# A mixed mLSTM and forgetting-attention step on one core: forget pages issued by GpSimd inside the q/k stage, one weight group rounded a step sooner, last outputs stored as whole rows

## The chip, the cores and the metric

The kernel runs on one core of a Trainium2 chip. The metric is the device time of one execution in microseconds; the median of the timed runs is compared. Engines are named as the profile names them: PE is TensorE (PEld its weight loads), DVE is VectorE, ACT is ScalarE, POOL is GpSimd, SP is SyncE (SPq its queue of DMA issues).

## The reference

One inference step of a two-layer decoder: an mLSTM layer and a layer of forgetting attention, each followed by a SwiGLU FFN, all in float32, for a prompt of 1024 positions (with 16 meta tokens ahead) and a decode batch of 8 x 8 positions. Cut to what the change touches:

```python
def mlstm_mixer(xn, C0, n0, m0, lead, w_in, b_ig, b_fg, mh_g, w_out):
    p = xn @ w_in                       # q | k | v | output gate | input gate | forget gate
    ...
    li = softcap(gi.astype(f32) + b_ig.astype(f32)).transpose(0, 2, 1)
    lf = jax.nn.log_sigmoid(softcap(gf.astype(f32) + b_fg.astype(f32))).transpose(0, 2, 1)
    h, state = mlstm_sequence(q, k, v, li, lf, state0, lead)
    h = rmsnorm(h.transpose(0, 2, 1, 3), mh_g)
    out = (h.reshape(B, T, HV).astype(xn.dtype) * jax.nn.sigmoid(og)) @ w_out
    return out, state
...
y = rmsnorm(h, prm['norm_final'])
```

The attention layer reads, for the decode batch, a paged cache: `page_table` (8 x 4) gives the pages of `cache_k`, `cache_v` and `cache_logf`; a page of `cache_logf` is 128 positions x 16 heads of log-forget values, whose running sums enter the attention scores.

## The kernel before

Positions form 9 tiles (`TT`: 80, then 8 of 128) and three groups of tiles (`TG`: 336, 384, 384 columns). Float32 products are made of three matmuls of a fast type: weights and activations are split into a high part (rounded by ACT, `whi`, `xh`) and a low part (the rest, by DVE, `wlo`, `xl`), and `mm3` (L193 to L195) multiplies high x high, high x low and low x high.

**The values stage** (`values_a`) is written out by hand: TensorE, SyncE, DVE and ACT run in the order of the code. Its loop over `i` has 9 + `LAG` steps, `LAG` = 5. Step `i` multiplies tile `i` by the weights of column group 0 (`values(0, i)`), and, from step 5 on, tile `i` - 5 by those of group 3 (`values(3, i - 5)`, 272 columns: 256 of v and 16 of the gates). `fetch(c, z)` loads half `z` of group `c` (`wraw`), `halve(c, z, ks)` rounds the quarters `ks` of that half: for each an ACT instruction (L665) and a DVE one (L666), and behind the last quarter of a half of group 3 the split of the gates' columns `gw` (L271, L272). Group 3's four pairs of quarters are rounded in steps 2 to 5.

**The q/k stage** (`phase_a`) has 24 steps `x`, one for each of 8 blocks of 128 columns of w_in and each group of positions. A step is 24 matmuls into `mmA` (a pool of two banks), an eviction by ACT into one of three buffers `stg` (L921), and a store to `qkD` from GpSimd's queue (L922). Each block's weights are loaded by SyncE (`load_w`, L256), rounded by ACT (L259) and DVE (L260). Between the steps stand:
- `rec_prep`, the work on the gates' rows: behind step 1 and behind step 4 TensorE transposes rows (`rps`, L1101, two banks) that ACT copies (`li`, `lf`, L1103); the rows of step 4 start a chain over DVE (scans `bA`, `mA`), ACT and DVE again, with stores from GpSimd: `out_p_m`, `out_s_m` (L1114, L1115), `eD` (L1120), and at its end `wD` (L1128). Behind step 9 TensorE transposes the results (`tps`, L1143, `wps`, L1147 and L1148).
- `cache_loads`: the page table is loaded, 32 registers are filled from it (L1011), and 32 pages of `cache_logf` are loaded by SyncE (L1013), four to a yield.
- `cache_prep`, at step 14: TensorE transposes the pages (`csps`, L1024), ACT copies (L1025), DVE sums (L1027), and GpSimd stores eight times `csE` (L1030). The loads of the state (`C`, `n`, L1308, L1310) wait for those stores.
- `wo_out`, at steps 6, 9, 12, 15 and 18: a block of w_out is loaded, rounded and stored (`woD`, L878) from GpSimd's queue.

Here TensorE alone runs in the order of the code; the order of the other engines is found by a scheduler when the program is built, and the registers of the pages are filled at the head of SyncE's program.

**The end** (`Tail`): the last three tiles of y_prompt are transposed back into two banks each, scaled by ACT (right half) and DVE (left half) and stored by SyncE in six stores of 128 x 512; the source of a store is four pieces of 128 columns of `H`.

## Time and profile before

| what | value |
|---|---|
| median of 3 timed runs | 2831.09 us (2831.01 to 2832.83) |
| profiled execution | 2833.03 us, of which the span is 2831.2 us |
| mean granted clock of TensorE | 0.994 |
| TensorE busy | 2760.9 us, 98% |
| DVE, ACT, POOL busy | 63%, 42%, 30% |
| DMA moved | 474.03 MB, mean 167 GB/s |

A row of a timeline gives start and duration in us, then the engine, the line, the operation, what is written and what is read, and in brackets the idle time ahead of it with what ended it. TensorE's durations overlap (matmuls are pipelined), so the distance between two starts tells what a matmul costs. A row of stretches (windows) gives for each engine the busy time in us with the number of instructions, then the clock that TensorE was granted (1.00 is full), the busy share of the DMA engines and GB/s. A row of waits says who waited on whom: us in total, times, the longest. A row of one line gives count and shortest, median and longest duration in ns, and when the first and the last began. Registers, waits and DMA issues don't count as busy.

### The profile page before, as it was taken

How to read it: one execution, taken by the hardware profiler on the slowest of the kernel's cores; microseconds unless marked ns; L12 is line 12 of the kernel's file. 1: busy time of each engine (PE TensorE's matmuls, PEld its weight loads, DVE VectorE, ACT ScalarE, POOL GpSimd, SP SyncE). 2: the span in 40 equal slices, each digit the busy share in tenths (PEclk: the TensorE clock that was granted, in tenths of full speed). 3: DMA queues.
4: the chain of work that ended last, by engine and by line, in shares of the span. 5: the costliest groups of instructions: out<-in, count | busy, mean ns of one | idle time of the engine just before them, and what ended most of it. 6: DMA issues, size and time to landing. Idle time of an engine off the chain costs nothing. (4 is left out here: it accounts for less than half of the span.)

```text
span 2831.2 us, 60542 instructions
## 1 busy us (share of the span) xinstructions
PE 2760.9 (98%) x23543; PEld 2649.8 (94%) x23543; DVE 1797.8 (63%) x4025; ACT 1177.0 (42%) x2299; POOL 837.0 (30%) x1316
## 2 busy tenths in 40 slices
PE   8989999999999999999999999999999999999998
PEld 8989889999999999999999888777899999999998
DVE  4632565888887665563455444777388888765656
ACT  5422453432322333443444445777343323323345
POOL 3122233132332332124352202554313223323111
PEclk9989999999999999999999999999999999999999
DMA  6666547245554375545443676442524555527556
GB/s 197 170 186 172 144 125 254 91 145 164 174 172 144 115 247 171 194 143 174 139 170 131 234 277 227 153 143 86 157 80 131 175 174 165 161 90 233 182 194 214
DMA packets 438737, 474.03 MB, mean 167 GB/s; under 512 B 41158, under 2 KB 364994, under 8 KB 437426
## 3 DMA queue, kind: packets, MB, share of 16 engines
q1 hardware_dynamic: 388050, 321.30, 36.9%
q0 software_dynamic: 43904, 143.18, 15.3%
q10 hardware_dynamic: 6496, 5.68, 0.6%
q8 instruction: 185, 3.03, 0.5%
q14 instruction: 102, 0.84, 0.1%
HBM read 322.84 MB, written 147.21 MB: 166 GB/s over the span
## 5 line engine op out<-in xcount | busy, mean ns | idle before, releaser
L1614 PE MATMUL m<-xh,slot 128*128 128x276 f32 x2752 | 540.5, 290 | 1.8 <-ACT fs L1643 1.8
L1614 PEld LDWEIGHTS m<-xh,slot 128*128 128x128 f32 x2752 | 439.6, 188 | 3.6 <-ACT fs L1643 2.2
L1614 PE MATMUL m<-xl,slot 128*128 128x276 f32 x1376 | 397.1, 289 | 0.0
L1614 PEld LDWEIGHTS m<-xl,slot 128*128 128x128 f32 x1376 | 258.7, 188 | 0.0
L193 PE MATMUL tmps<-slot,xh 128*128 128x256 f32 (+2 forms) x864 | 243.1, 281 | 0.0
L195 PE MATMUL tmps<-slot,xl 128*128 128x256 f32 (+2 forms) x864 | 240.6, 278 | 0.0
L194 PE MATMUL tmps<-slot,xh 128*128 128x256 f32 (+2 forms) x864 | 240.5, 278 | 0.0
L272 DVE TENSOR_TENSOR slot<-slot,slot 128x1024 fp32r<-128x1024 f32 x124 | 162.7, 1313 | 61.3 <-ACT slot L271 59.6
L271 ACT CAST slot<-slot 128x1024 fp32r<-128x1024 f32 x124 | 129.5, 1045 | 140.9 <-PE m L1614 111.7
L194 PEld LDWEIGHTS tmps<-slot,xh 128*128 128x128 f32 (+1 forms) x864 | 159.2, 184 | 0.1
L195 PEld LDWEIGHTS tmps<-slot,xl 128*128 128x128 f32 (+1 forms) x864 | 158.6, 184 | 0.0
L193 PEld LDWEIGHTS tmps<-slot,xh 128*128 128x128 f32 (+1 forms) x864 | 158.4, 183 | 0.2
L193 PE MATMUL mmA<-xh,whi 128*128 128x384 f32 (+1 forms) x384 | 135.7, 353 | 0.0
L194 PE MATMUL mmA<-xl,whi 128*128 128x384 f32 (+1 forms) x384 | 128.6, 335 | 0.0
L195 PE MATMUL mmA<-xh,wlo 128*128 128x384 f32 (+1 forms) x384 | 128.2, 334 | 0.0
L272 DVE TENSOR_TENSOR slot<-vA,slot 128x1024 fp32r<-128x1024 f32 (+1 forms) x59 | 82.2, 1396 | 32.6 <-ACT slot L271 31.5
L272 DVE TENSOR_TENSOR slot<-Ht,slot 128x1024 fp32r<-128x1024 f32 (+1 forms) x59 | 82.0, 1393 | 32.7 <-ACT slot L271 31.6
L271 ACT CAST slot<-Ht 128x1024 fp32r<-128x1024 f32 (+1 forms) x59 | 60.9, 1036 | 95.5 <-PE m L1614 86.5
L271 ACT CAST slot<-vA 128x1024 fp32r<-128x1024 f32 (+1 forms) x59 | 60.8, 1035 | 95.5 <-PE m L1614 86.5
L1718 DVE TENSOR_TENSOR ws<-ws 128x128 f32<-128x128 f32 x264 | 93.7, 355 | 8.9
L2865 ACT ACTIVATE s<-s,nb 128x272 f32<-128x272 f32 (+7 forms) x126 | 98.9, 786 | 0.0
L2900 ACT COPY th<-tp 128x768 f32<-128x768 f32 (+1 forms) x80 | 73.6, 920 | 53.6 <-PE tp L2892 30.5
(808 smaller groups left out, 8665.9 us busy)
## 6 DMA issues: line engine op xcount, KB each, us to landing
ws<-in_w_down SPq DMA_DIRECT2D x176, 128.0 KB, 2.7
sD<-ws SPq DMA_DIRECT2D x176, 128.0 KB, 2.2
slot<-sD SPq DMA_DIRECT2D x40, 512.0 KB, 4.4
slot<-in_w_gate_up SPq DMA_DIRECT2D x36, 512.0 KB, 3.9
kp<-in_cache_k SPq DMA_DIRECT2D x32, 512.0 KB, 6.2
vp<-in_cache_v SPq DMA_DIRECT2D x32, 512.0 KB, 5.1
vA<-in_w_gate_up SPq DMA_DIRECT2D x26, 512.0 KB, 4.5
Ht<-in_w_gate_up SPq DMA_DIRECT2D x26, 512.0 KB, 3.9
```

Of the source, the lines that this page charges most:

```text
L193: mm(ps, sh, mh, start=first, stop=False)
L194: mm(ps, sh, ml, start=False, stop=False)
L195: mm(ps, sl, mh, start=False, stop=last)
L271: self.nc.scalar.copy(hi, src)
L272: self.nc.vector.tensor_tensor(out=lo, in0=src, in1=hi.bitcast(F32), op=ALU.subtract)
L1614: nc.tensor.matmul(u.ps[h, b], w[p][:, k], x[q][:, k], start=first and k == i == 0, stop=k == 3 and i == 2, skip_group_check=True)
L1718: tt(out=o, in0=a, in1=b, op=ALU.subtract)
L2865: nc.scalar.activation(ss[z, u], ss[z, u], AF.Exp, bias=nb[:, z : z + 1], accum_out=sm[:, u, z : z + 1])
L2900: nc.scalar.copy(th.rearrange("p x z (u h q) -> p h (x z u) q", h=2, q=64)[:, :, :n], pt[:, :, :n])
```

## The change

Four edits. Lines in the following are those of the kernel after the change where an instruction has moved by a few lines (the eviction L921 becomes L922, its store L922 becomes L923).

1. `values_a`: group 3's pairs of quarters are rounded in steps 1 to 4, not 2 to 5.
2. `cache_loads`: the pages of `cache_logf` are loaded from GpSimd's queue, each behind a register load of GpSimd's own, two to a yield, from step 1 on (so in steps 1 to 16); GpSimd runs in the order of the code in this stage too; `cache_prep` moves from step 14 to step 18.
3. `page_at`: SyncE's registers for the pages of `cache_k` and `cache_v` are filled where they are first asked for. In the built program they stand where they stood, at the head of SyncE's queue.
4. `Tail.out`: the last three tiles are scaled into whole rows of 1024 and stored in one store each, two from SyncE's queue and the third from ACT's.

```diff
--- before.py
+++ after.py
@@ -791,8 +791,8 @@
                 keep(i + 2)
             if i + 6 < NT:
                 load(i + 6)
-            if 2 <= i < 6:
-                halve(3, i // 2 - 1, range(2 * (i % 2), 2 * (i % 2) + 2))
+            if 1 <= i < 5:
+                halve(3, (i - 1) // 2, range(2 * (1 - i % 2), 4 - 2 * (i % 2)))
             if i == 5:
                 fetch(1, 0)
                 fetch(1, 1)
@@ -882,6 +882,7 @@
 @_add(Net)
 def phase_a(self, vt):
     nc, I, O = self.nc, self.I, self.O
+    E = mybir.EngineType
     w_in = I["w_in_a"][0]
     qkD = self.dram.tile([8, P, T], F32, name="qkD")
     ogD = self.dram.tile([8, P, T], F32, name="ogD")
@@ -923,15 +924,16 @@
                     yield
 
         with self.pool("rowsA") as rp, self.pool("rowsAp", bufs=2, space=PSUM) as rpp, \
-                self.pool("cp") as cp, self.tc.manual_schedule(engines={mybir.EngineType.PE}):
+                self.pool("cp") as cp, self.tc.manual_schedule(engines={E.PE, E.Pool}):
             pages = self.cache_loads(cp)
             prep = self.rec_prep(kp, gates, rp, rpp)
             next(prep)
             for x, _ in enumerate(qk_out()):
                 if x in (1, 4, 9):
                     next(prep, None)
-                next(pages, None)
-                if x == 14:
+                if x:
+                    next(pages, None)
+                if x == 18:
                     self.cache_prep(*self.cache, rpp, "r")
                 if x % 3 == 0 and 5 < x < 21:
                     wo_out()
@@ -1002,16 +1004,14 @@
     nc, I = self.nc, self.I
     self.csE = self.dram.tile([NB, P, PAST], F32, name="csE")
     nc.sync.dma_start(self.ptab, I["page_table"].rearrange("b n -> (b n)").unsqueeze(0))
-    self.pages = []
+    self.pages = {}
     a, b = (cp.tile([P, 2 * PAST], F32, name=f"cp{x}") for x in range(2))
     lp = a[:, : NPG * NB * HB].rearrange("p (n b h) -> p n b h", n=NPG, b=NB)
-    for b_ in range(NB):
-        for n in range(NPG):
-            j = b_ * NPG + n
-            v = nc.sync.value_load(self.ptab[0:1, j : j + 1], min_val=0, max_val=I["cache_k"].shape[0] - 1)
-            self.pages.append(v)
-            nc.sync.dma_start(lp[:, n, b_, :], I["cache_logf"][bass.DynSlice(v, 1)].rearrange("a p h -> (a p) h"))
-        yield
+    for j in range(NB * NPG):
+        v = nc.gpsimd.value_load(self.ptab[0:1, j : j + 1], min_val=0, max_val=I["cache_k"].shape[0] - 1)
+        nc.gpsimd.dma_start(lp[:, j % NPG, j // NPG, :], I["cache_logf"][bass.DynSlice(v, 1)].rearrange("a p h -> (a p) h"))
+        if j % 2:
+            yield
     self.cache = lp, a[:, PAST:], b[:, :PAST], b[:, PAST:]
 
 
@@ -2063,17 +2063,11 @@
 
     def out(self, x, lo, hi):
         net, i = self.net, DONE[3][x]
-        nc, t0, t1 = net.nc, *TT[i]
-        for g, ps in enumerate((lo, hi)):
-            o = net.H[:, 4 * g : 4 * g + 4, t0:t1]
-            y, rr = ps.rearrange("p (k n) -> p k n", k=4), self.r[:, 1, x : x + 1]
-            if g:
-                nc.scalar.activation(o, y, AF.Copy, scale=rr)
-            else:
-                nc.vector.scalar_tensor_tensor(out=o, in0=y, scalar=rr, in1=net.sq[:, :512].rearrange(
-                    "p (k n) -> p k n", k=4), op0=ALU.mult, op1=ALU.mult)
-            nc.sync.dma_start(net.O["y_prompt"][0, (i - 1) * P : i * P, g * 512 : g * 512 + 512].rearrange(
-                "p (k n) -> p k n", k=4), o)
+        nc, rr = net.nc, self.r[:, 1, x : x + 1]
+        y = net.H[:, x, :D]
+        nc.scalar.activation(y[:, 512:], hi, AF.Copy, scale=rr)
+        nc.vector.scalar_tensor_tensor(out=y[:, :512], in0=lo, scalar=rr, in1=net.sq[:, :512], op0=ALU.mult, op1=ALU.mult)
+        (nc.scalar if x == 2 else nc.sync).dma_start(net.O["y_prompt"][0, (i - 1) * P : i * P], y)
 
     def finish(self, acc, groups):
         net = self.net
@@ -2494,12 +2488,21 @@
 
 
 @_add(Net)
+def page_at(self, j):
+
+    if j not in self.pages:
+        self.pages[j] = self.nc.sync.value_load(self.ptab[0:1, j : j + 1], min_val=0,
+                                                max_val=self.I["cache_k"].shape[0] - 1)
+    return self.pages[j]
+
+
+@_add(Net)
 def load_page(self, sk, b):
 
     self.page[b] = []
     for n in range(NPG):
         p = sk.tile([P, D], F32, name=f"kp{b}{n}", tag="kp", bufs=4)
-        self.nc.sync.dma_start(p, self.I["cache_k"][bass.DynSlice(self.pages[b * NPG + n], 1)].rearrange(
+        self.nc.sync.dma_start(p, self.I["cache_k"][bass.DynSlice(self.page_at(b * NPG + n), 1)].rearrange(
             "a p h d -> (a p) (h d)"))
         self.page[b].append(p)
 
@@ -2528,7 +2531,7 @@
         vp = []
         for n in range(NPG):
             p = s2.tile([P, D], F32, name=f"vp{b}{n}", tag="vp", bufs=6)
-            nc.sync.dma_start(p, I["cache_v"][bass.DynSlice(self.pages[b * NPG + n], 1)].rearrange(
+            nc.sync.dma_start(p, I["cache_v"][bass.DynSlice(self.page_at(b * NPG + n), 1)].rearrange(
                 "a p h d -> (a p) (h d)"))
             vp.append(p)
         Q = qb[b % 2]
```

What the order becomes on the engines. ACT in the values stage, in steps 4 and 5 (`xin` is the square of the rows of a later tile, `vA` an eviction, the last one that of group 3's first tile, `gw` the gates' columns), before:

```order
L751 ACTIVATE xin6_283,ss_136<-xin6_283 128x1024
L752 ACTIVATE rr_135<-ss_136,eps_67 128x1
L665 ACTIVATE whi_31_489<-wraw_14_260,gain_69 128x256 x2
L271 CAST xh_91<-xps_34_521 128x4x128
L271 CAST xh_91<-xps_35_526 128x4x128
L683 ACTIVATE vA_96<-tmps_33_495,rr_135 128x2x128
L751 ACTIVATE xin7_332,ss_136<-xin7_332 128x1024
L752 ACTIVATE rr_135<-ss_136,eps_67 128x1
L665 ACTIVATE whi_31_489<-wraw_14_260,gain_69 128x256 x2
L271 CAST whi_31_489<-gw_159 128x4x16
L683 ACTIVATE vA_96<-tmps_38_558,rr_135 80x2x128
```

and after:

```order
L751 ACTIVATE xin6_283,ss_136<-xin6_283 128x1024
L752 ACTIVATE rr_135<-ss_136,eps_67 128x1
L665 ACTIVATE whi_28_442<-wraw_14_260,gain_69 128x256 x2
L271 CAST whi_28_442<-gw_159 128x4x16
L271 CAST xh_91<-xps_34_527 128x4x128
L271 CAST xh_91<-xps_35_532 128x4x128
L683 ACTIVATE vA_96<-tmps_33_501,rr_135 128x2x128
L751 ACTIVATE xin7_332,ss_136<-xin7_332 128x1024
L752 ACTIVATE rr_135<-ss_136,eps_67 128x1
L683 ACTIVATE vA_96<-tmps_38_558,rr_135 80x2x128
```

The last rounding of group 3 (with `gw`) stood directly ahead of the first eviction of group 3; now it stands a step earlier, ahead of the two casts of `xh`.

ACT in the q/k stage about step 4 (`stg_112` and `stg_114` are the evictions of steps 3 and 4, `lf` the copies of the forget rows, `whi_133` the rounded fourth block of w_in), before:

```order
L259 CAST whi_126_2429<-wraw_125_2428 128x1024
L921 ACTIVATE stg_107_2053<-mmA_106_2028 128x384
L921 ACTIVATE stg_112_2127<-mmA_111_2102 128x336
L259 CAST whi_133_2534<-wraw_132_2533 128x1024
L921 ACTIVATE stg_114_2195<-mmA_113_2170 128x384
L1103 COPY lf_1870<-rps_115_2198 8x336
L1103 COPY lf_1870<-rps_116_2203 8x384
L1103 COPY lf_1870<-rps_117_2208 8x384
L1130 ACTIVATE stk_2230<-mA_1872 8x1104
```

and after:

```order
L259 CAST whi_126_2269<-wraw_125_2268 128x1024
L922 ACTIVATE stg_107_1993<-mmA_106_1968 128x384
L922 ACTIVATE stg_112_2047<-mmA_111_2022 128x336
L922 ACTIVATE stg_114_2095<-mmA_113_2070 128x384
L1103 COPY lf_1870<-rps_115_2098 8x336
L1103 COPY lf_1870<-rps_116_2103 8x384
L1103 COPY lf_1870<-rps_117_2108 8x384
L1130 ACTIVATE stk_2130<-mA_1872 8x1104
L259 CAST whi_133_2374<-wraw_132_2373 128x1024
```

The rounding of `whi_133` stood ahead of step 4's eviction and of the copies; now it stands behind them and behind `stk`.

GpSimd behind step 4's store (`cp` takes the pages, `ptab` is the page table, an ISA row works on registers), before:

```order
L922 DMA qkD<-stg_2195 128x384
L1115 DMA out_s_m<-mA 8x8x1
L1114 DMA out_p_m<-mA 8x1
L878 DMA woD_2599<-whi_2594 128x1024
L1120 DMA eD<-eA 8x1104
L922 DMA qkD<-stg_2311 128x384
L922 DMA qkD<-stg_2385 128x336
L1128 DMA wD<-wA 8x1104
L878 DMA woD_2599<-wlo_2595 128x1024
```

and after:

```order
L923 DMA qkD<-stg_2095 128x384
L1114 DMA out_p_m<-mA 8x1
L1115 DMA out_s_m<-mA 8x8x1
L1120 DMA eD<-eA 8x1104
L1128 DMA wD<-wA 8x1104
L1011 TENSOR_LOAD ptab
L1011 ISA x2
L1012 ISA
L1012 DMA cp_1946<-in_cache_logf 128x16
...
L923 DMA qkD<-stg_2191 128x384
```

The store `wD` now stands ahead of the stores of steps 5 and 6, and each step's pages stand between that step's store and the next one's. On SyncE the 32 page rows vanish, and the loads of w_in and w_out that stood behind them follow the earlier ones directly; on TensorE only the transposes `csps` move, four steps later.

## The prediction

> **What bounds the kernel now.** I read the page first. Its busy shares say that TensorE is the limit almost everywhere, so only what makes TensorE wait, or run slowly, can be won.
>
> ```profile
> PE 2760.9 (98%) x23543; PEld 2649.8 (94%) x23543; DVE 1797.8 (63%) x4025; ACT 1177.0 (42%) x2299; POOL 837.0 (30%) x1316
> ```
>
> The view of waits, asked for the first 46 us and for 140 to 255 us, gives two long waits of TensorE where the diff works: 2.7 us on ACT at L193, and 7.1 us on ACT at L1101. Both stand in the timelines below. The third place is the end of the program.
>
> **Part 1, group 3's weights a step sooner.** The timeline of TensorE at that wait, then two stretches of it (busy us of TensorE, its weight loads, DVE, ACT and GpSimd, then the granted clock and the DMA share):
>
> ```profile
> 34.82 0.29 PE L193 MATMUL tmps<-whi,xh 128*80 128x272 f32 x1
> ...
> 35.07 0.29 PE L195 MATMUL tmps<-whi,xl 128*80 128x272 f32 x1
> 38.11 0.51 PE L193 MATMUL tmps<-whi,xh 128*80 128x272 f32 x1 [2.75 <-ACT whi L271]
> ...
> 39.16 0.43 PE L193 MATMUL tmps<-whi,xh 128*80 128x272 f32 x1
> ...
> 39.62 0.43 PE L195 MATMUL tmps<-whi,xl 128*80 128x272 f32 x1
> ...
> 44.20 0.30 PE L195 MATMUL tmps<-whi,xl 128*128 128x256 f32 x1
> ```
>
> ```profile
> 20.00:24.00 4.00, 4.00 (x38) 4.00 (x37) 2.94 (x7) 3.17 (x8) 1.86 (x3) 1.00 0.98 326
> ...
> 40.00:44.00 4.00, 4.00 (x21) 4.00 (x20) 0.00 (x0) 0.63 (x2) 0.00 (x0) 0.50 0.26 77
> ```
>
> TensorE waits 2.75 us for the last quarter of the second half's weights, rounded in the same step that reads them. Behind it the granted clock is 0.50 (second stretch). Two starts take 0.46 us there (39.16 to 39.62) against 0.25 ahead of the wait (34.82 to 35.07). From 38.11 to 44.20, 6.1 us, the cold clock costs 6.1 x (1 - 0.25/0.46) = 2.8 us. Wait and cold clock together are 5.5 us.
>
> Rounded a step sooner, the weights are ready a step's length sooner, and what is added to step 1 must fit there (first stretch). ACT's roundings of two steps:
>
> ```profile
> 33.54 0.90 ACT L665 ACTIVATE whi<-wraw,gain 128x256 fp32r<-128x256 f32 x2
> ...
> 37.03 0.89 ACT L665 ACTIVATE whi<-wraw,gain 128x256 fp32r<-128x256 f32 x2
> ```
>
> A step is 3.5 us (33.54 to 37.03), more than the wait of 2.75. ACT is busy 3.17 of 4 us about step 1 and takes 0.89 more, DVE 2.94 and about as much: just full, without reserve. I leave 0.3 us of wait: **-5.2** (bounds 0, if the wait only moves, and -5.5).
>
> **Part 2, the pages off SyncE's queue.** The timelines of SyncE, ACT and TensorE at the 7.11 us wait:
>
> ```profile
> 130.63 18.31 SPq L1013 DMA_DIRECT2D cp<-in_cache_logf  x32
> 149.05 0.39 SPq L256 DMA_DIRECT2D wraw<-in_w_in_a  x1
> ```
>
> ```profile
> 153.31 1.04 ACT L259 CAST whi<-wraw 128x1024 fp32r<-128x1024 f32 x1 [9.56 <-DMA wraw<-in_w_in_a]
> ...
> 155.95 0.47 ACT L1103 COPY lf<-rps 8x384 f32<-8x384 f32 x1 [0.52 <-PE rps L1101]
> ```
>
> ```profile
> 147.21 0.78 PE L1101 MATMUL rps<-ident,lf_tm 80*8 80x80 f32 x6
> 155.11 0.80 PE L1101 MATMUL rps<-ident,lf_tm 128*8 128x128 f32 x3 [7.11 <-ACT lf L1103]
> ...
> 156.03 0.52 PE L194 MATMUL mmA<-xl,whi 128*128 128x384 f32 x1
> ...
> 156.99 0.52 PE L194 MATMUL mmA<-xl,whi 128*128 128x384 f32 x1
> ...
> 160.41 0.34 PE L193 MATMUL mmA<-xh,whi 128*128 128x384 f32 x1
> ...
> 160.93 0.34 PE L193 MATMUL mmA<-xh,whi 128*128 128x384 f32 x1
> ```
>
> SyncE issues 32 pages in a row for 18.31 us. The load of w_in behind them starts at 149.05, and ACT, whose next instruction is the rounding of that load, stands 9.56 us. The eviction of step 4 and the copies of the forget rows, which TensorE waits for, are queued behind it. After the change the load follows its predecessor directly, and on ACT the copies stand ahead of that rounding, so both causes go. What is late next is ACT's own eviction and first copies, done some 0.2 us after TensorE has its transposes: 6.9 of the 7.11 us go. The cold stretch goes with them: three matmuls take 0.96 us in it (156.03 to 156.99), 0.52 warm (160.41 to 160.93), so the 5.3 us from 155.11 to 160.41 cost 5.3 x (1 - 0.52/0.96) = 2.4. Together **-9.3** (bounds 0 and -9.5).
>
> **Part 3, the pages on GpSimd's queue: the unknown.** GpSimd now runs in program order: in step 4 it stops at the store of w (L1128), the end of a chain over DVE and ACT, and the remaining 26 pages, the qkD stores and the woD stores are queued behind. No page issue stands on GpSimd before, so I price it from rows of SyncE and of GpSimd's other DMAs:
>
> ```profile
> L922 POOL DMA_DIRECT2D qkD<-stg x24: 539/541/575, 132.6 to 242.5; - x24
> L1013 SPq DMA_DIRECT2D cp<-in_cache_logf x32: 332/333/1232, 130.6 to 148.6; - x32
> L1011 SPq TENSOR_LOAD <-ptab x9: 262/267/772, 38.2 to 43.6; - x9
> L1011 SPq TENSOR_LOAD <-ptab x32: 262/312/1044, 12.8 to 48.7; - x32
> DMA to landing us min/median/max: 1.6/1.8/3.8
> DMA to landing us min/median/max: 2.2/3.9/7.8
> ```
>
> The timelines of GpSimd, TensorE, ACT and SyncE further on:
>
> ```profile
> 167.65 0.80 POOL L1128 DMA_DIRECT2D wD<-wA  x1 [0.45 <-ACT wA L1127]
> 181.51 0.59 PE L1148 MATMUL wps<-tmA,selS 64*128 64x8 f32 x2
> 221.38 0.45 ACT L921 ACTIVATE stg<-mmA 128x336 f32<-128x336 f32 x1 [2.47 <-issue]
> 225.05 2.17 SPq L1310 DMA_DIRECT2D n<-in_state_n  x4
> 251.81 0.24 PE L1317 MATMUL n0p<-ident,n 32*128 32x32 f32 x1
> ```
>
> The two landing rows are the pages' (L1013) and the qkD stores' (L922). A GpSimd issue takes 0.54 us. A page adds registers, 18.31/32 - 0.333 = 0.24 on SyncE, and a register load, (43.6 - 38.2)/8 = 0.675 apart there. A page would cost 1.45 us. The low end is 0.54 + 0.24 + 0.26 = 1.04, with the shortest load and nothing behind it; the high end 2.2, if every load took the longest, 1.044 for the usual 0.3.
>
> Who waits: the transposes of the pages, now behind step 18 on TensorE, whose eviction is the row at 221.38. On the time axis of before, w goes out 11.2 us after the last copy of the rows (156.42 to 167.65). That copy now ends at about 148.9 (147.21 and 0.78 for the first transposes, 0.9 for the last group and its copy), so GpSimd is free again at 160.9. Until the last page it issues 26 pages, 12 qkD stores and 8 woD stores: 26p + 20 x 0.54. The page lands 1.8 us later. TensorE reaches the transposes at 221.38 less 9.3 and the 0.4 of the old transposes, 211.7. So there is no wait up to p = (211.7 - 1.8 - 160.9 - 10.8)/26 = **1.47 us**, and each 0.1 us above it costs 2.6 us. My value, 1.45, sits on that edge; I take **0** (bounds 0 and 26 x 0.73 = 19, with another 2.3 where the wait lets the clock fall). The evictions have three staging buffers. The first store after the stop, step 5's, is issued at 160.9 + 2.9 + 0.54 = 164.3 and lands at 168.2, at worst at 172.1; TensorE needs the next eviction from its buffer at 172.8, when it is through the small matmuls (181.51 + 0.6 - 9.3). That just holds. The csE stores and the state loads that wait for them come four steps later, some 4 x 8 x 0.52 = 16.6 us; the last state loads, issued until 227.2, are then issued at 243.8 and first used at 251.81, so their landing is hidden by 8 us, and if not, TensorE waits at L1317 for the rest.
>
> Beside this, GpSimd's DMAs land later while DVE is busy, as the store out_s_m shows, which was issued during the scans (its timeline and landing, the windows view, and a rounding on DVE):
>
> ```profile
> 157.30 0.61 POOL L1115 DMA_DIRECT2D out_s_m<-mA  x1 [1.72 <-DVE mA L1112]
> DMA to landing us min/median/max: 7.4/7.4/7.4
> 156.00:160.00 4.00, 4.00 (x14) 4.00 (x14) 4.00 (x8) 0.42 (x1) 0.61 (x1) 0.50 0.66 184
> 154.38 1.23 DVE L260 TENSOR_TENSOR wlo<-wraw,whi 128x1024 fp32r<-128x1024 f32 x1 [12.64 <-ACT whi L259]
> ```
>
> With DVE busy 4.00 of 4.00 us, 64 values take 7.4 us to land, against 2.2 to 3.9 for most 128x384 stores (L922 above), though the issue stays at 0.61. In the page steps DVE is idle most of the time. The Trainium skill ("SBUF — State Buffer", section "SBUF: two separate sides") says that a DMA issued from GpSimd starves while DVE runs an operation in a two-port mode, since GpSimd can't write its descriptors, and advises the SP or ACT queue. The landing time agrees, the issue time doesn't show it; by that rule the last page would land later by up to one rounding on DVE (1.23 us), and the gain would be up to 1.2 us smaller, 2816.6.
>
> **Part 4, the tail.**
>
> ```profile
> 2822.42 2.07 DVE L2073 SCALAR_TENSOR_TENSOR Ht<-fin,tr,sq 128x512 f32<-128x512 f32 x3
> 2823.06 4.13 SPq L2075 DMA_DIRECT2D out_y_prompt<-Ht  x6
> ```
>
> ```profile
> 2825.00:2826.00 1.00, 0.00 (x0) 0.00 (x0) 0.00 (x0) 0.00 (x0) 0.00 (x0) 0.50 1.01 285
> 24.00:28.00 4.00, 4.00 (x37) 4.00 (x37) 2.47 (x6) 3.18 (x7) 0.85 (x1) 1.00 1.02 395
> ```
>
> The DMA engines are full (1.01) at 285 GB/s for the last six stores: three tiles of 128 x 4 KB, 1.57 MB, in 5.5 us. Whole rows of 4 KB may move at the best rate that I saw, 395 GB/s: 4.0 us. The first store starts at most 0.3 later, since it needs both halves, DVE's (2.07/3 = 0.69) and ACT's beside it. **-1.2** (bounds +0.3, at the same rate, and -1.5).
>
> **Sum.** -5.2 - 9.3 + 0 - 1.2 = -15.7. The profiled execution took 2833.03 us, 1.8 beside its span and 1.9 above the median of the timed runs, 2831.09. So 2817.3 for such an execution, and 2815.4 for the median.
>
> **Rivals.** (a) *GpSimd is somewhat late*, p = 1.55 to 1.76: TensorE waits 2 to 7.5 us at the page transposes and runs cold behind it (+2.3): 2820 to 2825.4. For it: my price is on the edge, and register loads on a busy chip reached 1.044 us. Against it: issue times on GpSimd hardly vary (539 to 575 ns). (b) *The gain is used up*: p = 1.76 to 2.2, within 0.2% of before. (c) *Slower*: GpSimd's queue becomes the bound of the q/k stage, at two pages per step of some 4 us (8 x 0.52). It decides from p = 2.2 on, where 26 x 0.73 + 2.3 is past the gain plus 0.2%; at p = 2.5 the price is 26 x 1.03 + 2.3 = 29, so 2844.5. For it: nothing of the load's time on GpSimd has been seen. Against it: the nearest rows add to 1.45. (d) *Another cold stretch goes as well*, that behind the small transposes at 181.51: these are unchanged, so I give it little: if it costs what the two above do, 2.4 to 2.8, 2813. (e) *The first wait does not close*, since ACT and DVE are full in the steps: 2821.
>
> **How the numbers follow.** Forecast 0.48, (a) 0.20, (b) 0.09, (c) 0.11, (d) 0.05, (e) 0.07. A measurement of this kernel tells about 0.2%, 5.7 us, from no change. Faster: 0.48 + 0.20 + 0.05 + 0.07 = 0.80; same 0.09; slower 0.11. The range takes in (a), (d), (e) and the edge of (b): 2811.5 to 2828.
>
> **What would show it.** Right: no wait of TensorE at L193 near 38 and at L1101 near 150, clock near 1.00 in both places, pages at about 1.4 us each on GpSimd, and a last stretch of stores at over 350 GB/s. Wrong: a wait of TensorE at the page transposes with GpSimd's page issues as the last releaser (rivals a to c, told apart by the spacing of the pages); an eviction of qkD that waits for its buffer; a wait at L193 that has only moved.

## The result, and the profile after

The changed kernel takes **2819.12 us** (median of 15 runs, 2814.16 to 2823.09), the kernel before beside it on the same chips 2829.74 (median of 15, 2823.23 to 2833.84). The ratio is 0.9962, with an interval of 0.9955 to 0.9968: 9 to 13 us faster. The forecast was 2815.4, and 2811.5 to 2828 for the range; the sign and the range are right, and of the 15.7 us that the sum promised 10.6 came. (1.35 us of the distance to 2815.4 is the starting point: the sum set out from 2831.09, the median of three runs, and the 15 runs have 2829.74.) The profiled execution of after took 2820.11 us, with a span of 2818.5, against 2833.03 and 2831.2 before: 12.7 us of span, to be accounted for below.

The busy line of the page of after, first:

```profile
PE 2762.3 (98%) x23543; PEld 2650.7 (94%) x23543; DVE 1798.8 (64%) x4025; ACT 1177.1 (42%) x2299; POOL 856.1 (30%) x1348
```

The work is the same; GpSimd has 32 more instructions and 19 us more (32 page issues of 0.54, and other spans that are a little longer). What changed is where TensorE waits. Its view of waits over the first 460 us of after (in total, times, longest), of which two rows matter:

```profile
PE nps L1453 <- ACT vA L1423: 3.3, 3, 2.1
...
PE n0p L1317 <- DMA n<-in_state_n: 1.7, 1, 1.7
```

The wait at L193 near 38 us isn't there any more, and the one of 7.1 us at L1101 has shrunk to 0.3 (below, in TensorE's timeline). But a new one of 1.7 stands at L1317, and the longest wait at L1453 was 1.0 us before. The two places that the prediction spoke of, by stretches (busy us of TensorE, weight loads, DVE, ACT, GpSimd; granted clock; DMA share), and the row at L1101 in TensorE's timeline:

```profile
32.00:36.00 4.00, 4.00 (x36) 4.00 (x35) 3.86 (x10) 3.97 (x10) 1.57 (x2) 1.00 1.07 357
36.00:40.00 4.00, 4.00 (x37) 4.00 (x36) 1.34 (x4) 1.51 (x5) 0.86 (x1) 1.00 0.87 263
40.00:44.00 4.00, 4.00 (x35) 4.00 (x34) 2.55 (x5) 3.24 (x8) 0.42 (x1) 1.00 1.05 269
...
144.00:148.00 4.00, 4.00 (x26) 4.00 (x25) 4.00 (x3) 0.22 (x1) 0.00 (x0) 1.00 0.00 0
```

```profile
142.01 0.49 PE L1101 MATMUL rps<-ident,lf_tm 128*8 128x128 f32 x3 [0.32 <-ACT lf L1103]
```

The clock stays at 1.00 where it was 0.50, and the 4 us from 40 on now hold 35 matmuls, where before has 21. DVE and ACT are full in 32 to 36 (3.86 and 3.97 of 4), as feared, but they are on time. GpSimd's timeline and two of its lines show the pages:

```profile
154.10 0.82 POOL L1128 DMA_DIRECT2D wD<-wA  x1 [3.12 <-ACT wA L1127]
155.31 0.57 POOL L1012 DMA_DIRECT2D cp<-in_cache_logf  x1 [0.39 <-issue]
...
200.50 0.54 POOL L1012 DMA_DIRECT2D cp<-in_cache_logf  x1 [0.65 <-issue]
```

```profile
L1011 POOLq TENSOR_LOAD <-ptab x32: 284/300/752, 128.5 to 199.3; - x32
...
L1012 POOL DMA_DIRECT2D cp<-in_cache_logf x32: 537/537/571, 130.1 to 200.5; - x32
...
DMA to landing us min/median/max: 1.8/3.0/5.5
...
L1024 PE MATMUL csps<-ident,cp x4: 272/272/273, 204.3 to 204.6; 128*128 128x128 f32 x4
```

From the end of the store of w (154.92) to that of the last page (201.04) are 46.1 us; less 20 other issues of 0.545 and 1.0 us of idle time that a page didn't cause, 26 pages took **1.32 us** each (forecast 1.45, break-even 1.47). The last page is issued 3.8 us before TensorE comes to the transposes at 204.3, which don't wait: by 0.8 us at the median landing time of 3.0.

The new wait is at L1317. SyncE's timeline about the state loads, before and then after:

```profile
218.15 6.86 SPq L1308 DMA_DIRECT2D C<-in_state_C  x8
...
237.71 0.37 SPq L1282 DMA_DIRECT2D qk<-qkD  x1
```

```profile
217.06 3.68 SPq L1308 DMA_DIRECT2D C<-in_state_C  x4
223.40 0.38 SPq L1282 DMA_DIRECT2D qk<-qkD  x1
223.82 4.50 SPq L1308 DMA_DIRECT2D C<-in_state_C  x4
228.36 2.12 SPq L1310 DMA_DIRECT2D n<-in_state_n  x4
```

TensorE's rows, the page transposes in before and the rest in after, and the stretches around the wait:

```profile
205.00 0.60 PE L1024 MATMUL csps<-ident,cp 128*128 128x128 f32 x4
```

```profile
237.21 0.21 PE L1317 MATMUL n0p<-ident,n 32*128 32x32 f32 x1 [1.73 <-DMA n<-in_state_n]
...
242.10 0.52 PE L195 MATMUL mmA<-xh,wlo 128*128 128x384 f32 x1
242.42 0.52 PE L193 MATMUL mmA<-xh,whi 128*128 128x384 f32 x1
```

```profile
228.00:232.00 4.00, 4.00 (x36) 3.67 (x36) 0.32 (x1) 2.67 (x3) 0.54 (x1) 1.00 1.18 215
232.00:236.00 4.00, 3.48 (x22) 3.10 (x20) 2.79 (x5) 0.49 (x1) 0.70 (x2) 1.00 1.11 247
236.00:240.00 4.00, 2.79 (x16) 2.35 (x18) 0.97 (x3) 0.00 (x0) 0.58 (x1) 0.84 0.60 178
240.00:244.00 4.00, 4.00 (x22) 3.67 (x19) 0.05 (x1) 0.75 (x2) 3.01 (x6) 0.50 0.19 50
```

The state loads are the last of a block of DMAs that fills the engines (shares of 1.18 and 1.11). The n loads are issued until 230.48, TensorE wants them at 235.48 and gets them at 237.21: 6.7 us after the issue. In before the load of qk (L1282) stands behind the whole block of state loads; in after it stands between the fourth and the fifth load of C. Behind the wait the clock falls to 0.50, and matmuls start 0.32 us apart instead of 0.17.

The tail, one stretch of the last stores:

```profile
2813.50:2814.50 1.00, 0.00 (x0) 0.00 (x0) 0.00 (x0) 0.00 (x0) 0.00 (x0) 0.50 1.02 401
```

Whole rows go out at 401 GB/s; the half rows of before, gathered from pieces of 128 values, went at 285.

**Where TensorE stands against before.** For each kernel I took the first start of a line (the views by line) and subtracted it from that of before; negative is earlier, in us. The profiled executions are single ones. The kernels e1 to e11 are those of the next section.

| kernel | L1101 | L1143 | L1352 | L1317 | L1441 | L1453 | L1558 | last matmul | span |
|---|---|---|---|---|---|---|---|---|---|
| before, at | 133.8 | 177.7 | 246.3 | 251.8 | 259.9 | 323.4 | 408.1 | 2821.9 | 2831.2 |
| after | -6.3 | -15.0 | -16.4 | -14.6 | -13.8 | -13.8 | -12.0 | -11.7 | -12.7 |
| after again (e9) | -7.4 | -16.2 | -16.2 | -15.0 | -14.7 | -13.0 | -11.2 | -15.4 | -16.4 |
| part 1 alone (e1) | -6.6 | -7.5 | -8.9 | -8.8 | -8.9 | -8.8 | -8.9 | -11.4 | -11.4 |
| pages alone (e2) | -1.1 | -9.9 | -11.3 | -9.8 | -9.6 | -7.9 | -4.3 | -2.8 | -2.7 |
| tail alone (e3) | -1.0 | -1.3 | -1.2 | -1.2 | -1.2 | -1.2 | -1.2 | -2.2 | -3.9 |
| parts 1 and 4 (e10) | -6.4 | -6.4 | -9.4 | -9.4 | -9.4 | -7.8 | -7.8 | -7.6 | -9.3 |
| transposes at step 17 (e4) | -4.7 | -13.6 | -13.3 | -13.2 | -13.8 | -13.7 | -13.8 | -15.2 | -16.3 |
| pages in step 4, transposes at 17 (e11) | -5.6 | -14.4 | -14.5 | -14.4 | -14.9 | -14.9 | -14.9 | -19.5 | -20.5 |

The pages and the tail alone are 1 us early at L1101 too, where nothing of theirs has happened: that much is scatter of the start. Between L1143 and L1352 the kernels of the table gain from -0.3 (e4, with a wait of its own) and 0 (e3, e9, e11) to 1.5 us, and e10 3.0; e1 (1.4) and e10 don't touch the pages, so this is scatter too. It is the cold stretch behind the small transposes: the clock is 0.59 and 0.55 in the 8 us from 180 in before, 0.88 and 0.69 in the 8 us from 164 in after, 0.58 and 0.57 there in e9, and in e10 there is none. After stands 16.4 us ahead by L1352, gives 2.6 back by L1441 and 1.8 more by L1558.

### The profile page after: what moved, and what is told of

Its sections match the earlier page's. It is cut to its first block, busy times and chain, and to the rows that moved or that the text cites. A ratio compares the mean times of both kernels' runs of the same rounds, so it can differ in the third digit from the quotient of the medians.

```text
span 2818.5 us, 60631 instructions
## 1 busy us (share of the span) xinstructions
PE 2762.3 (98%) x23543; PEld 2650.7 (94%) x23543; DVE 1798.8 (64%) x4025; ACT 1177.1 (42%) x2299; POOL 856.1 (30%) x1348
## 5 line engine op out<-in xcount | busy, mean ns | idle before, releaser
L193 PE MATMUL tmps<-slot,xh 128*128 128x256 f32 (+2 forms) x864 | 243.1, 281 | 0.0
L193 PEld LDWEIGHTS tmps<-slot,xh 128*128 128x128 f32 (+1 forms) x864 | 158.4, 183 | 0.2
L193 PE MATMUL mmA<-xh,whi 128*128 128x384 f32 (+1 forms) x384 | 135.2, 352 | 0.1
```

The source lines that it names most:

```text
L193: mm(ps, sh, mh, start=first, stop=False)
```

## The experiments

Twelve kernels, in three groups, each on one chip with its own runs of before: medians 2829.38 (e1, e2, e3, e5), 2829.52 (e4, e6, e7, e8) and 2827.96 (e9 to e12). Lines shift by one to three where an edit adds some; names are those of each kernel's own page.

**e1, group 3's weights alone** (edit of before):

```
-            if 2 <= i < 6:
-                halve(3, i // 2 - 1, range(2 * (i % 2), 2 * (i % 2) + 2))
+            if 1 <= i < 5:
+                halve(3, (i - 1) // 2, range(2 * (1 - i % 2), 4 - 2 * (i % 2)))
```

> Edit 1 alone in the kernel before. Theory (the weights of group 3 were rounded too late, and the clock falls behind the wait): the 2.7 us wait of TensorE at L193 near 38 us and the half clock behind it both go, and the q/k stage starts 5 to 6.5 us earlier, as in the changed kernel; the 7.1 us wait at L1101 stays, shifted: 5 to 6.5 us less than before at the end of the program. Rival (the wait only moves, or is given back by the loads, which DMA paces): the first evictions of the q/k stage lie less than 2 us earlier than before, and the time is within 2 us of before.

Measured: 2821.3, ratio 0.9970 (0.9959 to 0.9982). The wait at L193 is gone, TensorE stands 6.6 us ahead at L1101, and the second wait is untouched in its view of waits:

```profile
PE rps L1101 <- ACT lf L1103: 7.1, 1, 7.1
```

So part 1 closes its gap by itself. The time fell by 8 us, more than its place shows; the table has 2.5 us of it after L1558, where nothing was edited.

**e2, the pages alone** (after, with the edit of group 3's weights and of the tail undone):

```
-            if 1 <= i < 5:
-                halve(3, (i - 1) // 2, range(2 * (1 - i % 2), 4 - 2 * (i % 2)))
+            if 2 <= i < 6:
+                halve(3, i // 2 - 1, range(2 * (i % 2), 2 * (i % 2) + 2))
...
```

> Edits 2 and 3 alone (pages on GpSimd's queue). Theory: the wait at L193 near 38 us stays 2.7, the wait at L1101 falls from 7.1 to under 0.5 us with no half clock behind it, step 18's eviction lies 9 to 10 us earlier than before, and 2 to 4 us of that are given back where the transpose of the state rows (L1317) waits for the loads of n, which stand behind the csE stores: 5 to 8 us less than before. Rival (nothing is given back there, the loss against the forecast is the clock's chance alone): no wait at L1317 and 9 to 10 us less.

Measured: 2824.51, ratio 0.9982 (0.9973 to 0.9991), 4.9 us less. Its view of waits:

```profile
PE nps L1453 <- ACT vA L1423: 3.6, 3, 2.4
...
PE n0p L1317 <- DMA n<-in_state_n: 1.4, 1, 1.4
```

The wait at L193 is there, with 3.5 us. The table gives 8.8 us between L1101 and L1143, as in after (8.7), and 7.0 lost between L1352 and L1558. Both late waits of after are there without part 1 and without the tail: they come with the pages' edits.

**e3, the tail alone** (edit of before):

```
-        for g, ps in enumerate((lo, hi)):
...
+        (nc.scalar if x == 2 else nc.sync).dma_start(net.O["y_prompt"][0, (i - 1) * P : i * P], y)
```

> Edit 4 alone. Theory (whole rows of 4 KB move faster than pieces of 512 bytes): from the last matmul to the end of the span 1 to 1.5 us less than before, the stretch of stores at 350 GB/s or more. Rival (the rate is set by something else, such as the issue or the landing of the last store): the rate stays at 285 GB/s, or rises without the end moving, and the time is within 0.3 us of before.

Measured: 2826.16, ratio 0.9987 (0.9978 to 0.9997). A stretch behind its last matmul:

```profile
2822.00:2823.00 1.00, 0.00 (x0) 0.00 (x0) 0.24 (x1) 0.00 (x0) 0.00 (x0) 0.50 1.02 418
```

From the first scaling to the span's end are 7.2 us, against 8.85 before and 7.85 in after: 1.0 to 1.65 us. The rest of the 3.2 us by the medians lies ahead of the tail, where this kernel is the one before.

**e5, the n loads ahead of the C loads.** Is it only the place of the n loads at the block's end that costs?

```
+    for j in range(4):
+        nc.sync.dma_start(n0[j * 8 : j * 8 + 8], I["state_n"][0, 2 * j : 2 * j + 2].rearrange("a h k -> h a k"))
...
-    for j in range(4):
-        nc.sync.dma_start(n0[j * 8 : j * 8 + 8], I["state_n"][0, 2 * j : 2 * j + 2].rearrange("a h k -> h a k"))
```

> The changed kernel with the four small loads of n issued ahead of the eight of C on SyncE. Theory (TensorE waits 1.7 us at L1317 only because the loads of n stand last in a queue that starts four steps later): the wait at L1317 goes, the clock stays at 1.00 from 236 to 248 us, and the attention of the decode batch starts 3 to 4 us earlier than in the changed kernel: 3 us less than the changed kernel, unless the wait for C takes its place. Rival (the loads of C land as late and TensorE waits for them at L1441, or the clock falls there for another reason): less than 1 us.

Measured: 2818.96, ratio 0.9961 (0.9948 to 0.9975): the time of after. The wait at L1317 is gone, and TensorE's timeline has another:

```profile
245.28 1.28 PE L1441 MATMUL nps<-C,qq 128*80 128x129 f32 x8 [3.75 <-POOL C L1398]
```

Before waits 2.1 us at this place. So the wait moved to the next use of the late block; the order of the loads in it wins nothing, as the rival said. Six loads of C stand behind the load of qk here, on SyncE's queue.

**e4, the transposes a step sooner**, in step 17:

```
-                if x == 18:
+                if x == 17:
```

> The changed kernel with the page transposes (cache_prep) at step 17, not 18. Theory (GpSimd has no slack: the last page is issued at 201.0 and lands some 3 us later, just when TensorE is through step 18): TensorE waits 2 to 4 us at the page transposes; csE and the state loads come as much earlier as the wait leaves, so the wait at L1317 shrinks: within 3 us of the changed kernel either way. Rival (the pages have room, and only the place of csE decides): no wait at the page transposes, no wait at L1317, and 3 us less than the changed kernel.

Measured: 2815.14, ratio 0.9951 (0.9936 to 0.9966), some 4 us below after, though the intervals overlap (four runs). From its view of waits:

```profile
PE csps L1024 <- DMA cp<-in_cache_logf: 1.3, 1, 1.3
```

The step sooner does cost a wait for the pages, 1.3 us, so no slack worth a step was there. But the wait at L1317 is gone, and the longest at L1453 is 1.0 again. In the table e4 is 3 us behind after at L1352 and 1.8 ahead of it at L1558. The n loads, in SyncE's timeline, are not sooner for it in absolute time, but later:

```profile
230.48 1.71 SPq L1310 DMA_DIRECT2D n<-in_state_n  x4
```

They are out at 232.19, and TensorE comes for them at 238.57, 3.1 us later than in after (its start is 1.6 later, and it has waited 1.3): 6.4 us of margin instead of 5.0. The n loads don't follow the transposes a step forward because the load of qk stands ahead of them: it goes out at 228.73, after a wait of 7.5 us for a store to qkD, and behind it stand two loads of C, where after has four.

**e6, the page's register loaded twice**, which makes a page dearer and nothing else:

```
+        nc.gpsimd.value_load(self.ptab[0:1, j : j + 1], min_val=0, max_val=I["cache_k"].shape[0] - 1)
```

> The changed kernel with the register of every page loaded twice on GpSimd, which adds some 0.6 us to a page (1.32 us measured between the stop at the store of w and the last page). Theory (GpSimd's queue is on the edge, 26 pages stand behind that stop, each 0.1 us costs 2.6): TensorE waits at the page transposes or at the staging buffers for 12 to 18 us in all, the clock falls there, and the time is 10 to 20 us more than the changed kernel: at or past the kernel before. Rival (the queue has room that the program order hides, or loads overlap): less than 4 us more.

Measured: 2830.24, ratio 1.0003 (0.9994 to 1.0013): the gain is used up. From its view of waits, GpSimd's timeline and one stretch of the wait:

```profile
PE csps L1025 <- DMA cp<-in_cache_logf: 12.7, 4, 4.8
```

```profile
154.36 0.82 POOL L1129 DMA_DIRECT2D wD<-wA  x1 [3.13 <-ACT wA L1128]
...
216.68 0.54 POOL L1013 DMA_DIRECT2D cp<-in_cache_logf  x1 [1.84 <-issue]
```

```profile
212.00:216.00 4.00, 0.45 (x1) 0.18 (x1) 0.42 (x1) 1.04 (x1) 1.25 (x3) 0.50 0.83 313
```

A page takes (217.22 - 155.18 - 10.9)/26 = 1.97 us. The prediction's rule, 2.6 us for each 0.1 above 1.47, makes that 13 us of wait, and 12.7 were measured. So the break-even and the slope of part 3, which this one kernel tests together, were right. After is nearer to the bound than its 0.15 us per page below the break-even says, 3.9 us in all: 0.8 us were left at the transposes at the median landing time, since the pages landed in 3.0 us and not in 1.8, GpSimd idled 1.0, and TensorE was there about 1 us sooner than the sum had it.

**e7, eight pages in step 4 ahead of the row work**, while GpSimd waits for the chain to w, and the transposes in step 15:

```
+                if x == 4:
+                    for _ in range(4):
+                        next(pages, None)
...
-                if x:
+                if x and x != 4:
...
-                if x == 18:
+                if x == 15:
```

> The changed kernel with eight pages, not two, in step 4 and ahead of the work on the rows, where GpSimd else stands idle for the chain of DVE and ACT; the last page then comes in step 13, and the page transposes stand at step 15. Theory (the gain of the change is given back where state loads wait for csE): the pages are done before the transposes, no wait at L1317, and the time from 230 to 300 us is as in the kernel before, shifted by 16 us: 2 to 5 us less than the changed kernel. Rival (what is given back is given back by the clock further on, whatever the state loads do): L1317 does not wait, but the time is within 1.5 us of the changed kernel.

Measured: 2815.73, ratio 0.9956 (0.9943 to 0.9970). That is 3 us further below its before than after is, with intervals that overlap. No wait at L1317, nor at the transposes: all state loads stand ahead of the load of qk here, and are out at 220.31. But they now come so early that they also stand ahead of a load of w_in, and ACT and TensorE wait for that:

```profile
227.92 1.04 ACT L259 CAST whi<-wraw 128x1024 fp32r<-128x1024 f32 x1 [9.81 <-DMA wraw<-in_w_in_a]
```

```profile
PE mmA L193 <- ACT stg L922: 3.5, 1, 3.5
```

That is the pattern of the wait that the change removed (a load of weights behind a block on SyncE's queue), with the block moved. The same block of DMAs can come too late for its first reader, or too early for the weights.

**e8, no pages at all**; the buffer is zeroed:

```
-    for j in range(NB * NPG):
...
+    nc.gpsimd.memset(a[:, : NPG * NB * HB], 0.0)
+    yield
```

> The changed kernel without the loads of the forget pages and their registers (the page buffer is set to zero instead, so the attention of the decode batch works with wrong log-forget values of the past). Theory (on GpSimd the pages are hidden; what costs is the place of csE): within 1.5 us of the changed kernel, with the wait at L1317 still there. Rival (the pages still cost on GpSimd, through late stores and evictions): 3 us less or more.

Measured: 2824.37, ratio 0.9984 (0.9975 to 0.9993), 5.2 us below its before where after is 10.6 below: without the pages some 5 us slower than with them, which neither theory had. From its view of waits:

```profile
PE tps L1140 <- DVE tmA L1141: 3.2, 1, 3.2
```

Without the pages the scheduled engines took another order: on DVE roundings now stand ahead of the copies that TensorE's small transposes wait for. So this kernel changes more than the pages, and it prices nothing. It shows one thing: the wait at L1317 is there too (1.3 us, in its own line), so GpSimd's time for the pages isn't needed for it.

**e9, after once more, e10, parts 1 and 4 without the pages.** Together they price the pages' edits on one chip.

```
-            if 2 <= i < 6:
-                halve(3, i // 2 - 1, range(2 * (i % 2), 2 * (i % 2) + 2))
+            if 1 <= i < 5:
+                halve(3, (i - 1) // 2, range(2 * (1 - i % 2), 4 - 2 * (i % 2)))
...
+        (nc.scalar if x == 2 else nc.sync).dma_start(net.O["y_prompt"][0, (i - 1) * P : i * P], y)
```

> The changed kernel once more, unchanged. Theory (two waits come with the change: at L1317 for the loads of n, and at L1453, where the load of eb lands late beside the first loads of woD; the rest of what the first profile lost is where the clock happens to fall): both waits are in this profile too, 1 to 2.5 us each, while the half clock near 1730 and 1800 us, where the change does nothing, is there only by chance. Rival (the clock falls at the same places every time, so the late losses belong to the change): half clock again near 1730 and 1800 us.

> Edits 1 and 4 without the pages' edits. Theory (the pages' edits gain 7 to 8 us against edit 1 alone by step 18 and then give much of it back at L1317, at L1453 and by the clock): 2818 to 2821 us, that is within 2 us of the changed kernel. Rival (what is given back is noise, the pages' edits are worth the 9 us forecast): 6 us or more above the changed kernel, 2825 or more.

Measured: e9 2815.38 (2813.7 to 2820.53), ratio 0.9962 (0.9949 to 0.9976), the ratio of after; e10 2823.8, ratio 0.9985 (0.9976 to 0.9994). e9's view of waits has the late ones again:

```profile
PE nps L1453 <- ACT vA L1423: 3.3, 3, 2.1
...
PE n0p L1317 <- DMA n<-in_state_n: 1.0, 1, 1.0
```

The wait at L1441 is 2.5 us here, where after has none. The pages' edits are worth 8.4 us by these medians, and 6.5 by the two ratios. I had come to think, from e1 (nearly all of the gain with one part), that they were worth within 2 us; that theory fell, and the rival (6 or more) held, though its 2825 us weren't reached. e1's time had been a lucky one, or e10's is an unlucky one: e1 gained 8.1 us on its chip, and e10, with the tail added to it, 4.2. The parts alone add up to 8.1 + 4.9 + 3.2 = 16.2 us, the whole to 10.6, so by medians a part is known to a few us only; what it does is told better by its waits.

**e11 and e12, six pages in step 4 ahead of the row work**, with the transposes in step 17 (e11) or 16 (e12):

```
+                if x == 4:
+                    for _ in range(3):
+                        next(pages, None)
...
-                if x:
+                if x and x != 4:
...
-                if x == 18:
+                if x == 17:
```

> The changed kernel with six pages in step 4 ahead of the work on the rows, so that the last page comes in step 14, and the page transposes at step 17. Theory (GpSimd's idle time in step 4 takes the pages, so neither the page transposes nor the loads of n make TensorE wait): no wait at L1024 and L1317, 4 to 6 us less than the changed kernel. Rival (the wait of the state's other chain, over GpSimd at L1441, or of eb at L1453, takes its place): within 2 us of the changed kernel.

> As the one before, with the page transposes at step 16. Theory: csE and the state loads 4 us earlier than there; since neither makes TensorE wait there, no gain: within 1 us of it. Rival (the loads of C, now all ahead of the load of q and k on SyncE, hold up q and k or a block of weights, as eight pages in step 4 with the transposes at step 15 did, where a block's load came late and TensorE waited 3.5 us for an eviction behind it): a new wait of 2 us or more, and 2 to 4 us more.

Measured: e11 **2812.26**, ratio 0.9952 (0.9938 to 0.9965), the lowest median of all; e12 2816.21, ratio 0.9962 (0.9949 to 0.9976). In e11 neither the transposes nor L1317 wait, and the longest wait at L1456 (L1453 of after) is 1.0. Its row at L1444 in the view of waits, its n loads in SyncE's timeline, and the stretches that were cold in after:

```profile
PE nps L1444 <- POOL C L1401: 1.6, 1, 1.6
```

```profile
229.10 1.64 SPq L1313 DMA_DIRECT2D n<-in_state_n  x4
```

```profile
236.00:240.00 4.00, 4.00 (x33) 3.46 (x32) 2.22 (x5) 0.49 (x1) 1.28 (x2) 1.00 0.76 222
240.00:244.00 4.00, 3.39 (x27) 2.93 (x21) 0.37 (x1) 1.24 (x3) 3.49 (x7) 1.00 0.26 68
```

Against e9 on the same chip e11 wins 3.1 us by the medians, where 4 to 6 were expected; with five runs each, 2810.55 to 2817.67 against 2813.7 to 2820.53, that isn't clear of the noise. The n loads are out at 230.74, no sooner than in after, and TensorE comes at 237.44: 6.7 us, as long as they take to land (6.7 in after and e9, 6.8 in e2). TensorE is 2 us later than in after, 0.7 by its start and 1.2 by a longer half clock about 164 to 172. But the n loads move with TensorE too: the load of qk ahead of them goes out at 226.67, when a store of TensorE's step 21 has landed, and three loads of C stand behind it. So absolute times don't tell whether the edit or the clock made the margin. Over the kernels it goes with the edit: with the transposes in step 17 or 16 (e4, e11, e12) it is 6.4 to 6.7 us, with step 18 (after, e9, e2, e8) 5.0 to 5.7; e6, step 18 behind its 12.7 us of waits, has 6.5. By the table e11 is 1.8 behind e9 at L1101, where nothing of the edit has run yet, level at L1441 (-14.9, -14.7), and 3.7 ahead at L1558: 1.8 of that at the load of eb, told of below, and the rest clock. e12, still a step sooner, has the wait for eb again and new ones:

```profile
PE nps L1456 <- ACT vA L1426: 3.6, 3, 2.4
...
PE sps L1355 <- DMA qk<-qkD: 1.4, 1, 1.4
```

So with six pages in step 4 the transposes did better in step 17 than in step 16; step 18 wasn't tried with them. The early loads of wo are in e12 and not in e11, so part of e11's lead is that of the eb load, which I had not planned.

## Why the prediction was right, and where it was not

- **Part 1, -5.2: right.** After stands 6.3 us ahead at L1101, of which the scatter of the start is 1.0 (e2 and e3 have it too): 5.3. (The other kernels with part 1 stand 4.7 to 7.4 ahead there, so the nearness to 5.2 is partly luck.) The wait closed although DVE and ACT are full. Rival (e) is out.
- **Part 2, -9.3: right.** 8.7 us between L1101 and L1143, which holds the wait and the cold stretch; e2 has 8.8, and so has e9. What is left of the wait is 0.3, not 0.2.
- **Part 3, the pages' price: right, at the edge as said.** 1.32 us for 1.45, and no wait at the transposes. That 1.47 is the break-even, and 2.6 us per 0.1 the slope, e6 shows. Rivals (a) to (c) describe kernels such as e6 (2830.24, rival (b)); they aren't this one.
- **Part 3, the state loads: the step that failed.** "Their landing is hidden by 8 us, and if not, TensorE waits at L1317 for the rest" was put at nothing in the sum. The 8 us come from moving the block of state loads by four steps, 16.6 us, as one piece. Counted from the page transposes (205.00 in before, 204.28 in after), TensorE is ready for L1317 after 31.2 us, where 46.8 - 16.6 = 30.2 were due; but the last n load is out after 26.2 us, where 22.2 were due. The 4 us are SyncE's. The block, moved by 16.6 us on the axis of before (to 234.7 and on), meets the load of qk, which stands at 237.71 there. In after that load stands behind the fourth C load and goes out at 223.40, 2.7 us after it (2.6 of them a wait for a store to qkD); what stands behind it comes only then (223.82, 228.36), and those four C loads take 4.50 us, where the eight of before took 6.86. So the margin was 5.0 us (8.0 - 4.0 + 1.0), and the landing took 6.7, at a DMA share of 1.11 to 1.18; 8 us would have hidden it.

  That the gain itself narrowed it is ruled out by e2: TensorE comes 5 us later there than in after, and the margin is 5.4. That the load of qk is the cause is read from the queue's rows, and from e7, where the state loads stand ahead of it; no run moved that load alone.

  Price: 1.7 of wait, and about 6.8 us at half clock (238.67 to 245.46), 6.8 x (1 - 0.173/0.32) = 3.1, less the 2.1 us that before waits at L1441 and after doesn't: 2.7, and the table has 2.6. Four kernels give the landing time: after, e9, e2 and e8, with margins of 5.0, 5.7, 5.4 and 5.2 us, wait 1.7, 1.0, 1.4 and 1.3, so 6.5 to 6.8 us. Those with margins of 6.4 (e4), 6.5 (e6) and 6.7 (e11, e12) don't wait.
- **Not in the sum: 1.8 us at L1453.** TensorE lost it near 389 us, where DVE stands for the load of eb; the rows of after, first DVE's, then TensorE's, SyncE's and that load's landing:

```profile
383.74 3.42 DVE L1335 SCALAR_TENSOR_TENSOR eb<-eb,tmA,cap 128x128 f32<-128x128 f32 x8 [1.45 <-DMA eb<-eD]
```

```profile
389.38 1.16 PE L1453 MATMUL nps<-vA,eb 128*128 128x129 f32 x8 [2.12 <-ACT vA L1423]
```

```profile
372.31 41.83 SPq L512 DMA_DIRECT2D wo<-woD  x8
...
DMA to landing us min/median/max: 7.0/7.9/8.8
```

The same two in e1, where those loads of wo start only after 400 us:

```profile
387.24 2.18 DVE L1335 SCALAR_TENSOR_TENSOR eb<-eb,tmA,cap 128x128 f32<-128x128 f32 x8
...
DMA to landing us min/median/max: 6.5/6.9/7.2
```

In after SyncE issues the first two loads of wo at 372.31, beside GpSimd's load of eb at 374.9, which then lands 8.8 us after its issue. The early loads and the wait of 2.1 to 2.6 us come together in after, e2, e5, e9 and e12, with e8 as a sixth, and in the other eight kernels there is neither. They go together in all fourteen kernels; that the loads cause the wait was not tried by itself, and why their buffers come free sooner stays open.
- **Part 4, -1.2: right.** 1.0 in after, up to 1.65 in e3, at the 400 GB/s that the sum used.
- **Rival (d)** came in part: the 1.4 us between L1143 and L1352 are the cold stretch behind the small transposes, shorter in after; since e9, the same kernel, gains nothing there, that is scatter.
- **What the sum makes now.** -1.0 (start) - 5.3 - 8.7 - 1.4 (clock between L1143 and L1352) + 2.6 + 1.8 + 0.3 (clock further on) - 1.0 = -12.7, the difference of the two spans. By the medians it is 10.6; the other 2 us lie within what single executions differ.
- **The rule on GpSimd's queue.** The Trainium skill ("SBUF — State Buffer", section "SBUF: two separate sides") speaks of a DMA from GpSimd that starves while DVE holds the port. The issues on GpSimd didn't get longer (537 to 571 ns), the landings did: 3.0 and at most 5.5 us for the pages, against 1.8 and 3.8 on SyncE. Whether DVE or the fuller DMA engines made that longer, no run tells apart; the transposes had 0.8 us to spare for it, so it cost nothing. The store out_s_m doesn't settle it either: in after it landed 8.6 us after its issue at 148.60, but out_p_m, issued at 148.04 in the same stretch with DVE busy 1.00 of 1 us, landed after 1.6.

## What to carry to other kernels

When a block of loads moves within an engine's queue, don't shift it as one piece: write the queue out as it will stand, with the loads that the block now meets, and ask what each of those waits for. Compare the margin that is left with a landing time from a stretch with the same DMA share, not from a quiet one, and count it from the reader's own position, since the start and the clock shift all absolute times. A queue that does just enough (1.32 us per page against a break-even of 1.47) can be priced in advance by its break-even, and a copy of the costly instruction tests that price in one run. Moving such work by a step trades one reader against the next, so the steps on both sides belong in the trial.

## What the runs showed of the hardware

- A register load and a DMA with an address from it take 1.32 us on GpSimd's queue: 0.54 for the issue, 0.30 at the median for the load, the rest between instructions. A second load of the same register adds 0.65.
- The clock fell behind a wait of 1.73 us in after (2.79 of 4 us busy), to 0.84, 0.50 and 0.80 in three stretches, some 6.8 us at half clock; in e11 a wait of 1.6 us at L1444 left the stretches around it at 1.00. The Trainium skill ("TensorE: Matmul & The Clock Gate", Part 1) puts the fall behind an idle window of some 3.4 us that runs free of the program. Here less idle time was enough, and which waits are answered by it differs; that the clock's windows run free fits, no more.
- So does the scatter: one program loses clock in other places from execution to execution. The same stretch in after and in e9, which is the same kernel (near 1732 both fall, and so do e10 and e12, but before, e1 and e11 don't):

```profile
1800.00:1804.00 4.00, 4.00 (x33) 2.48 (x32) 1.04 (x4) 0.49 (x1) 1.40 (x4) 0.50 0.15 39
```

```profile
1800.00:1804.00 4.00, 3.49 (x43) 2.54 (x45) 2.73 (x12) 1.56 (x4) 2.13 (x5) 1.00 0.21 64
```

Runs of the changed kernel go from 2814.16 us at a mean clock of 0.998 to 2823.09 at 0.993. That is 8.9 us for 0.005 of the clock, so a change of 5 us in this kernel needs many runs, and a profile pair alone can be off by as much (e2's profiled execution took 2830.05 us, its median is 2824.51).
- Stores of 4 KB rows filled the DMA engines at 401 GB/s in after and 418 in e3, those of half rows in pieces of 128 values at 285.
